# An encoder layer on one core: retention's values for two heads at a time, the heads' projections dealt anew, first loads on another queue, last store in two

## The chip, the cores and the metric

The kernel runs on one core of one Trainium2 chip. A core has a matrix engine (TensorE, PE in the profile; the loads of its stationary operand are shown as PEld), VectorE (DVE), ScalarE (ACT), GpSimd (POOL) and SyncE (SP). SP only issues DMA transfers here; ACT and POOL issue some beside their work. Each engine runs its own list of instructions in order, and semaphores tie the lists together. The metric is the time of one execution on the device in microseconds (us), lower is better, as the median of several runs.

## The reference, cut to what matters

Two request groups of 256 rows and 1024 features go through the same layer with shared weights: a token mixer of two branches (retention with 4 heads, latent attention with 8 heads), then a convolutional gated MLP. All is in float32. Of the mixer's input projection, the parts that the change deals with:

```python
h = _layernorm(x) * (1.0 + sc1) + sh1
proj = h @ w_in
rq, rk, rv, rg, dq, dkv, kr, gA, gB = jnp.split(proj, offs, axis=-1)
rq = _apply_rope(rq.reshape(B, S, RET_HEADS, RET_QK_DIM), cos_r, sin_r)
rk = _apply_rope(rk.reshape(...), cos_r, sin_r) * (RET_QK_DIM ** -0.5)
rv = rv.reshape(B, S, RET_HEADS, RET_V_DIM)          # 4 heads x 256
ro = _bidirectional_retention(rq, rk, rv, ret_decay_fwd, ret_decay_bwd)
ro = _layernorm(ro).reshape(B, S, RET_V_W) * ret_gn_g
y_a = (jax.nn.silu(rg) * ro) @ w_ret_o
merged = jax.nn.sigmoid(gA) * y_a + jax.nn.sigmoid(gB) * y_b
```

The layer ends with `x = _layernorm(ALPHA * x + (1 + g2) * y) * ln2_g + ln2_b`, which is stored. The vectors `sc1`, `sh1`, `g1` and so on are pieces of `silu(c) @ w_ada + b_ada`, where `c` is one row per group.

## The kernel before, in words

Both groups are treated as one matrix of T = 512 rows. The normalized and modulated input `hT` is held transposed: 8 tiles of 128 features x 512 rows (NK = 8). Every float32 operand of a large product is split into a rounded high part and a low rest (`split`, names ending in `_h` and `_l`): ScalarE casts the high part (L151), VectorE subtracts it (L141). A product is then three matmuls (`mm3`, L161 to L163).

Weights are loaded by SP in chunks of 128 x 2048 (1 MB) into two raw buffers (`w_raw`, L192), and split into two high and two low buffers (`w_split`). So a chunk's load waits for the split of the chunk before the last, and its split for TensorE's end with that chunk.

Retention runs in a stage of its own after the attention branch:

- `ret_proj(h)` for a head: a chunk `wqk` gives query and key (2 x 8 x 3 matmuls 512 wide, then `rope` and a split), a chunk `wrv` gives the values, a chunk `wrg` gives the gate (`ps_rg`, then Silu on ScalarE).
- For the values the rows are the stationary operand and the weights stream past: for each of 4 blocks of 128 rows and 8 k, `mm3` into 256 columns of a PSUM tile, one head's width. Two row blocks share a tile `ps_rv` of 512 columns.
- `ret_core(h)` is the head itself: scores (`ps_rs`) times decay gives `sd`, split into `sds`; times values gives `ps_ro`; statistics on VectorE (`lnr_st`), a power on POOL (`lnr_rs`), normalization on ScalarE (`ro`); one head later (for the last head at once) `ret_flip` transposes (`ps_rt`), multiplies with the gate (`rg`, L984) and splits into `roT`.

`interleave(main, filler, ratio)` writes down the steps of a core and, between them, pieces of a filler: the projections of the next head, and for the last head the columns of gate A (`gate_a`, `ps_ga`). Each step yields a cost, and the filler runs until its sum is `ratio` times that of the core. `with_later` also puts in, about every 5 units of cost, a piece of `later`: the adaptive vectors of the second half of the layer, computed on VectorE from loads `araw` (`acc`, L489 and L491) and summed by TensorE (`ps_sum`).

TensorE follows this written order. The order of the other engines, of SP's transfers too, is set by a scheduler from the same program; they then run it in order. PSUM has 8 tiles of 512 columns that all share.

After the last head come the products with `w_ret_o` (`ps_ya`, chunk `wro`); the first two of these take k = 0 to 5 first, and k = 6 and 7, the last head's `roT`, at the end.

At the start SP issues two loads of `c` (`c16`, L173 and L174), the bias rows `b_rows` (L178), then `x` in eight tiles (L223) and `w_ada` in pieces of 256 KB (`wada`, L229). TensorE first runs `ps_warm` matmuls on ones, the transposes `ps_c` of `c16s` and `b_rows`, 16 more `ps_warm`, and then the transposes of `x` (`ps_xt`) between `ps_ada`, products with `wada`. At the end, for each block of 128 rows, VectorE scales (L1383), scales and shifts (L1386) two tiles of 512 columns, and each is stored as it is ready, the first by SP, the second by ACT (L1387).

Of the kernel before, what the change touches and what calls it, by code (L numbers as in the profile page):

```python
# [109 lines left out]
def encoder_kernel(ctx: ExitStack, tc: tile.TileContext, ins, outs):  # L110
# [62 lines left out]
    nc.sync.dma_start(c16[0:8], ins["c_prompt"].rearrange("o (k p) -> (o k) p", p=128))  # L173
    nc.sync.dma_start(c16[8:16], ins["c_sample"].rearrange("o (k p) -> (o k) p", p=128))  # L174
# [3 lines left out]
    nc.sync.dma_start(b_rows, ins["b_ada"].rearrange("o (k p) -> (o k) p", p=128))  # L178
# [342 lines left out]
    with tc.manual_schedule(engines={PE}):  # L521
# [375 lines left out]
        ret = {}  # L897

        def ret_proj(h):
            def pieces(raw):  # L900
# [11 lines left out]
            wv = k_cols(w_in, 0, NK, OFF_RV + h * 256, 256, f"wrv{h}")
            v = []
            for tp in range(2):
                ps = ps512(f"ps_rv{h}_{tp}")
                for i in range(2):
                    t = 2 * tp + i
                    for k in range(NK):
                        mm3(ps[:, i * 256:(i + 1) * 256], cut(hT[k], slice(None), slice(t * 128, t * 128 + 128)),
                            cut(wv, slice(None), k), k == 0, k == NK - 1)  # L920
                v.append(split(ps, f"rv{h}_{tp}"))
                yield 5.2
            wg = k_cols(w_in, 0, NK, OFF_RG + h * 256, 256, f"wrg{h}")
            rg = []
# [12 lines left out]
        def ret_scores(h, g):  # L937
            q, k, _, _, dec = ret[h]
# [37 lines left out]
        def ret_flip(h):  # L976
            for e in range(2):
# [5 lines left out]
                rg = ret[h][3][e]  # L983
# [388 lines left out]
        for t in range(4):  # L1372
# [11 lines left out]
            for cc in range(2):  # L1384
                y = x2[t][cc]
                dve.scalar_tensor_tensor(out=y, in0=y, scalar=rs, in1=ln2b[cc], op0=ALU.mult, op1=ALU.add)  # L1386
                (nc.scalar if cc else nc.sync).dma_start(dst[:, cc * 512:(cc + 1) * 512], y)  # L1387
# [25 lines left out]
```

## Time and profile before

| what | us |
|---|---|
| runs shown | 868.7, 872.14, 1428.62 |
| their median | 872.14 |
| the profiled execution | 868.35 |
| its span in the profile | 866.5 |
| busy: TensorE, VectorE, ScalarE, POOL | 851.8, 612.2, 380.0, 93.3 |

The profile is one execution, recorded by the hardware. A row of a timeline reads: start, length, engine, line of the code, operation, output and inputs, shapes, count, and in brackets the idle time before it with what ended it. Matmuls overlap in the records, since a next one starts before the last has drained; their pace is read from the distance of starts. A row of grouped instructions gives count, total busy time, mean length in ns. In the chain of waits each piece has its start, its length and the engine or transfer that held the end at that moment.

### The profile page before, as it was taken

What the parts mean: (1) busy time and instruction counts of PE and PEld (TensorE: products, weight loads), DVE (VectorE), ACT (ScalarE), POOL (GpSimd) and SP (SyncE); (2) the same over time, 40 slices, a digit from 0 to 9 for tenths busy, and PEclk for the clock granted to TensorE, in tenths of its full rate; (3) what the DMA queues carried; (4) which work ended last, traced back from release to release, by engine and by line L of the source; (5) the groups of instructions that cost most, each with busy time, mean ns of one, the idle gap of its engine ahead of it and who ended that gap; (6) DMA issues with size and microseconds to landing.
All of it is one profiled execution on the core that took longest, in us unless ns stands there. A gap on an engine that the chain in (4) does not pass through costs nothing.

```text
span 866.5 us, 11686 instructions
## 1 busy us (share of the span) xinstructions
PE 851.8 (98%) x4401; PEld 720.8 (83%) x4401; DVE 612.2 (71%) x1051; ACT 380.0 (44%) x647; POOL 93.3 (11%) x141
## 2 busy tenths in 40 slices
PE   8999999999999999999999999999999999999996
PEld 5678888988889898988788899888888888888885
DVE  5465888884677787883986967578657756855666
ACT  3564877551343433453343166434433535443500
POOL 3031012362000000000010210000000000100100
PEclk9999999999999999999999999999999999999998
DMA  9943156799466425354358423245343464655731
GB/s 289 355 153 110 50 153 182 198 294 277 121 168 204 112 98 158 100 185 162 118 187 234 145 82 101 74 146 158 96 147 122 148 181 134 149 167 156 261 112 66
DMA packets 131528, 137.64 MB, mean 159 GB/s; under 512 B 8741, under 2 KB 100227, under 8 KB 131472
## 3 DMA queue, kind: packets, MB, share of 16 engines
q1 hardware_dynamic: 120864, 112.65, 41.5%
q0 software_dynamic: 9888, 23.14, 11.8%
q10 hardware_dynamic: 720, 1.11, 0.3%
q8 instruction: 34, 0.56, 0.3%
q14 instruction: 22, 0.18, 0.1%
HBM read 129.53 MB, written 22.03 MB: 175 GB/s over the span
## 4 chain that ended last, share of the span: by engine, by line
PE 91%; DVE 2%; ACT 2%; DMA 2%; issue 1%; SPq 1%; DVEq 0%; ACTq 0%
PE ps_b L161 5%; PE ps_b L163 5%; PE ps_b L162 5%; PE ps_a L162 5%; PE ps_a L163 5%; PE ps_a L161 5%; PE ps_d L163 4%; PE ps_d L162 4%; PE ps_d L161 4%; PE ps_rv L162 2%; PE ps_rv L163 2%; PE ps_rv L161 2%; PE ps_rqk L161 2%; PE ps_rqk L163 2%; PE ps_rqk L162 2%; PE ps_rg L161 2%
## 5 line engine op out<-in xcount | busy, mean ns | idle before, releaser
L491 DVE SCALAR_TENSOR_TENSOR acc<-araw,csil,acc 128x512 f32<-128x512 f32 x112 | 78.4, 747 | 19.8 <-DMA araw<-in_w_ada_dram 19.8
L161 PE MATMUL ps_b<-h_h,wup_h 128*128 128x512 f32 (+1 forms) x200 | 72.8, 364 | 0.3 <-ACT h2m L401 0.3
L162 PE MATMUL ps_a<-h_l,wup_h 128*128 128x512 f32 (+1 forms) x200 | 72.9, 365 | 0.1
L163 PE MATMUL ps_a<-h_h,wup_l 128*128 128x512 f32 (+1 forms) x200 | 72.8, 364 | 0.0
L161 PE MATMUL ps_a<-h_h,wup_h 128*128 128x512 f32 (+1 forms) x200 | 72.8, 364 | 0.0
L163 PE MATMUL ps_b<-h_h,wup_l 128*128 128x512 f32 (+1 forms) x200 | 72.7, 364 | 0.0
L162 PE MATMUL ps_b<-h_l,wup_h 128*128 128x512 f32 (+1 forms) x200 | 72.7, 364 | 0.0
L141 DVE TENSOR_TENSOR wup_l<-wup_r,wup_h 128x1024 fp32r<-128x1024 f32 (+1 forms) x46 | 52.7, 1173 | 10.2 <-ACT wup_h L151 9.4
L151 ACT CAST wup_h<-wup_r 128x1024 fp32r<-128x1024 f32 (+1 forms) x46 | 44.2, 1014 | 29.8 <-PE ps_b L162 20.2
L144 DVE TENSOR_TENSOR conv<-conv,ps_b 128x512 f32<-128x512 f32 x22 | 15.1, 686 | 40.6 <-PE ps_b L163 37.0
L161 PEld LDWEIGHTS ps_b<-h_h,wup_h 128*128 128x128 f32 x200 | 37.7, 189 | 6.4 <-ACT h2m L401 0.5
L162 PEld LDWEIGHTS ps_a<-h_l,wup_h 128*128 128x128 f32 x200 | 37.7, 189 | 6.2 <-DVE h_l L141 0.3
L163 PEld LDWEIGHTS ps_a<-h_h,wup_l 128*128 128x128 f32 x200 | 37.7, 189 | 6.2 <-DVE wup_l L141 0.3
L162 PEld LDWEIGHTS ps_b<-h_l,wup_h 128*128 128x128 f32 x200 | 37.7, 189 | 6.0
L163 PEld LDWEIGHTS ps_b<-h_h,wup_l 128*128 128x128 f32 x200 | 37.7, 189 | 5.9
L161 PEld LDWEIGHTS ps_a<-h_h,wup_h 128*128 128x128 f32 x200 | 37.7, 189 | 5.9
L162 PE MATMUL ps_rv<-wrv_l,h_h 128*128 128x256 f32 x128 | 36.2, 283 | 0.0
L163 PE MATMUL ps_rv<-wrv_h,h_l 128*128 128x256 f32 x128 | 36.2, 283 | 0.0
L161 PE MATMUL ps_rv<-wrv_h,h_h 128*128 128x256 f32 x128 | 36.2, 283 | 0.0
L1194 ACT ACTIVATE conv<-ps_a,vecs 128x512 f32<-128x512 f32 x22 | 17.1, 779 | 41.8 <-PE ps_a L163 41.8
L1196 DVE SCALAR_TENSOR_TENSOR conv<-ps_a,vecs,conv 128x510 f32<-128x510 f32 x22 | 16.4, 746 | 23.8 <-ACT conv L1194 23.8
L1200 ACT ACTIVATE conv<-conv 128x512 f32<-128x512 f32 x22 | 13.9, 631 | 40.7 <-DVE conv L1198 40.7
(383 smaller groups left out, 2480.6 us busy)
## 6 DMA issues: line engine op xcount, KB each, us to landing
wup_r<-in_w_up_dram SPq DMA_DIRECT2D x44, 512.0 KB, 5.3
araw<-in_w_ada_dram SPq DMA_DIRECT2D x64, 256.0 KB, 5.9
wsum<-in_w_down_dram POOLq DMA_DIRECT2D x42, 256.0 KB, 7.6
wada<-in_w_ada_dram SPq DMA_DIRECT2D x32, 256.0 KB, 6.3
w_r<-wsum SPq DMA_DIRECT2D x28, 256.0 KB, 3.7
wga_r<-in_w_in_dram SPq DMA_DIRECT2D x4, 1024.0 KB, 5.4
wmo_r<-in_w_mla_o_dram SPq DMA_DIRECT2D x4, 1024.0 KB, 5.2
wqk_r<-in_w_in_dram SPq DMA_DIRECT2D x8, 512.0 KB, 5.4
```

Of the source, the lines that this page charges most:

```text
L141: return (eng or dve).tensor_tensor(out=out, in0=a, in1=b, op=ALU.subtract)
L144: (eng or dve).tensor_tensor(out=out, in0=a, in1=b, op=ALU.mult)
L151: last_split.append(act.copy(hi, src).ins)
L161: pe.matmul(out, l[0], r[0], start=start, stop=False, skip_group_check=skip)
L162: pe.matmul(out, l[0], r[1], start=False, stop=False, skip_group_check=skip)
L163: pe.matmul(out, l[1], r[0], start=False, stop=stop, skip_group_check=skip)
L491: dve.scalar_tensor_tensor(out=acc[g], in0=raw, scalar=s, in1=acc[g], op0=ALU.mult, op1=ALU.add)
L1194: act.activation(a, pa, AF.Identity, scale=convw[:, 1, f:f + 1], bias=convb[:, f:f + 1])
L1196: dve.scalar_tensor_tensor(out=av_[:, :, 1:256], in0=pv[:, :, 0:255], scalar=convw[:, 0, f:f + 1], in1=av_[:, :, 1:256], op0=ALU.mult, op1 ...
L1200: act.activation(a, a, AF.Gelu)
```

## The change

- The values are computed for two heads in one go: `ret_value(h)` for h = 0 and 2 loads two chunks of 4 k x 512 columns (`wrv0_0`, `wrv0_4`), keeps four PSUM tiles open, one for each block of rows, and streams 512 columns, two heads' width, in each matmul. A tile of 128 rows x 512 is split, and each head later takes its 256 columns of it (`value_r`).
- `ret_proj` keeps query and key only; the gate is `ret_gate(h)`.
- What runs beside which head is dealt by a table `beside`. Before, head h had the whole projection of head h + 1, and the last head gate A's columns. Now the first core has query and key of head 1 and the gates of heads 1 and 2, the second query and key of head 2 and the values of heads 2 and 3, the third query, key and gate of head 3 and a chunk of gate A, the last two chunks of gate A. The ratios are 6.0, 6.0, 6.0 and 4.6 instead of 6.0 three times and 7.0.
- The two loads of `c` and that of `b_rows` are issued by ACT instead of SP.
- For the last block of rows the second 512 columns are finished and stored in two halves, the first stored by ACT, the second by SP.

```diff
-FILL_MLA, FILL_RET = 0.46, 7.0
+FILL_MLA, FILL_RET = 0.46, (6.0, 6.0, 6.0, 4.6)
...
-    nc.sync.dma_start(c16[0:8], ins["c_prompt"].rearrange("o (k p) -> (o k) p", p=128))
+    nc.scalar.dma_start(c16[0:8], ins["c_prompt"].rearrange("o (k p) -> (o k) p", p=128))
...
-            wv = k_cols(w_in, 0, NK, OFF_RV + h * 256, 256, f"wrv{h}")
-            v = []
-            for tp in range(2):
-                ps = ps512(f"ps_rv{h}_{tp}")
-                for i in range(2):
-                    t = 2 * tp + i
-                    for k in range(NK):
-                        mm3(ps[:, i * 256:(i + 1) * 256], cut(hT[k], slice(None), slice(t * 128, t * 128 + 128)),
-                            cut(wv, slice(None), k), k == 0, k == NK - 1)
-                v.append(split(ps, f"rv{h}_{tp}"))
-                yield 5.2
+            ret[h] = qk[0], qk[1], decay_tile(h)
+
+        def ret_value(h):
+
+            pss = [ps512(f"ps_rv{h}_{t}") for t in range(4)]
+            for k0 in (0, 4):
+                wv = k_cols(w_in, k0, 4, OFF_RV + h * 256, 512, f"wrv{h}_{k0}")
+                for t in range(4):
+                    for k in range(4):
+                        mm3(pss[t], cut(hT[k0 + k], slice(None), slice(t * 128, t * 128 + 128)),
+                            cut(wv, slice(None), k), k0 + k == 0, k0 + k == NK - 1)
+                    if k0:
+                        values[h, t] = split(pss[t], f"rv{h}_{t}")
+                    yield 2.7
+            for i in range(2):
+                value_r[h + i] = [cut(values[h, t], slice(None), slice(i * 256, i * 256 + 256)) for t in range(4)]
...
-        drain(with_later(ret_proj(0)))
+        drain(with_later(chain(ret_proj(0), ret_value(0), ret_gate(0))))
+        beside = [(ret_proj(1), ret_gate(1), ret_gate(2)), (ret_proj(2), ret_value(2)),
+                  (ret_proj(3), ret_gate(3), gate_a(range(EARLY_GA, 2))), (gate_a(range(2, 4)),)]
         for h in range(HR):
-            nxt = ret_proj(h + 1) if h + 1 < HR else gate_a(range(EARLY_GA, 4))
-            interleave(ret_core(h), with_later(nxt), 6.0 if h + 1 < HR else FILL_RET)
+            interleave(ret_core(h), with_later(chain(*beside[h])), FILL_RET[h])
...
-            for cc in range(2):
-                y = x2[t][cc]
-                dve.scalar_tensor_tensor(out=y, in0=y, scalar=rs, in1=ln2b[cc], op0=ALU.mult, op1=ALU.add)
-                (nc.scalar if cc else nc.sync).dma_start(dst[:, cc * 512:(cc + 1) * 512], y)
+            for cc, a, b in ((0, 0, 512), (1, 0, 512)) if t < 3 else ((0, 0, 512), (1, 0, 256), (1, 256, 512)):
+                y = x2[t][cc][:, a:b]
+                dve.scalar_tensor_tensor(out=y, in0=y, scalar=rs, in1=ln2b[cc][:, a:b], op0=ALU.mult, op1=ALU.add)
+                (nc.scalar if cc and not a else nc.sync).dma_start(dst[:, cc * 512 + a:cc * 512 + b], y)
```

How the order of instructions moves, at three places. The first is the head of the DMA lists. SP before (`x0_0` is the first tile of `x`):

```order
L173 DMA c16_77<-in_c_prompt_dram 8x128
L174 DMA c16_77<-in_c_sample_dram 8x128
L178 DMA b_rows_81<-in_b_ada_dram 48x128
L223 DMA x0_0_83<-in_x_prompt_dram 128x512
L223 DMA x0_1_85<-in_x_prompt_dram 128x512
```

ScalarE now, ahead of its first computation (the Silu of `c16`):

```order
L173 DMA c16_77<-in_c_prompt_dram 8x128
L174 DMA c16_77<-in_c_sample_dram 8x128
L176 DMA cst_72<-in_cst_dram 128x128
L178 DMA b_rows_81<-in_b_ada_dram 48x128
L280 ACT_TABLE_LOAD
L280 ACTIVATE c16s_192<-c16_77 16x128
```

The three small loads left SP's list, which now begins with `x0_0`, and stand around the load of `cst` in ScalarE's.

The second place is TensorE's first values, behind the key projection of head 0 (`h0` and `h1` are k = 0 and 1 of `hT`). Before:

```order
L163 MATMUL ps_rqk0_1_2559<-h7_h_657,wqk0_l_2510 128x512
L161 MATMUL ps_rv0_0_2611<-wrv0_h_2605,h0_h_363 128x256
L162 MATMUL ps_rv0_0_2611<-wrv0_l_2606,h0_h_363 128x256
L163 MATMUL ps_rv0_0_2611<-wrv0_h_2605,h0_l_364 128x256
L161 MATMUL ps_rv0_0_2611<-wrv0_h_2605,h1_h_377 128x256
```

and now:

```order
L163 MATMUL ps_rqk0_1_2559<-h7_h_657,wqk0_l_2510 128x512
L161 MATMUL ps_rv0_0_2606<-wrv0_0_h_2612,h0_h_363 128x512
L162 MATMUL ps_rv0_0_2606<-wrv0_0_l_2613,h0_h_363 128x512
L163 MATMUL ps_rv0_0_2606<-wrv0_0_h_2612,h0_l_364 128x512
L161 MATMUL ps_rv0_0_2606<-wrv0_0_h_2612,h1_h_377 128x512
```

Each value matmul streams 512 columns instead of 256; TensorE's list has 192 matmuls fewer in all.

The third place is VectorE at the last head, from the accumulation over `araw` to the low parts of `roT` that `ps_ya` takes last. Before:

```order
L491 SCALAR_TENSOR_TENSOR acc2_1_0_4267<-araw2_1_1_0_4312,csil_194,acc2_1_0_4267 128x512
L984 SCALAR_TENSOR_TENSOR rg3_0_3980<-ps_rt3_0_4357,vecs_235,rg3_0_3980 128x512
L491 SCALAR_TENSOR_TENSOR acc2_1_1_4268<-araw2_1_1_0_4312,csil_194,acc2_1_1_4268 128x512
L984 SCALAR_TENSOR_TENSOR rg3_1_4015<-ps_rt3_1_4367,vecs_235,rg3_1_4015 128x512
L141 TENSOR_TENSOR wro1_l_4388<-wro1_r_4385,wro1_h_4387 128x1024
L491 SCALAR_TENSOR_TENSOR acc2_1_0_4267<-araw2_1_1_1_4316,csil_194,acc2_1_0_4267 128x512
L141 TENSOR_TENSOR wro1_l_4388<-wro1_r_4385,wro1_h_4387 128x1024
L491 SCALAR_TENSOR_TENSOR acc2_1_1_4268<-araw2_1_1_1_4316,csil_194,acc2_1_1_4268 128x512
L141 TENSOR_TENSOR roT6_l_4364<-rg3_0_3980,roT6_h_4363 128x512
L141 TENSOR_TENSOR roT7_l_4374<-rg3_1_4015,roT7_h_4373 128x512
```

and now:

```order
L491 SCALAR_TENSOR_TENSOR acc2_1_0_4044<-araw2_1_1_0_4120,csil_194,acc2_1_0_4044 128x512
L491 SCALAR_TENSOR_TENSOR acc2_1_1_4045<-araw2_1_1_0_4120,csil_194,acc2_1_1_4045 128x512
L491 SCALAR_TENSOR_TENSOR acc2_1_0_4044<-araw2_1_1_1_4124,csil_194,acc2_1_0_4044 128x512
L491 SCALAR_TENSOR_TENSOR acc2_1_1_4045<-araw2_1_1_1_4124,csil_194,acc2_1_1_4045 128x512
L992 SCALAR_TENSOR_TENSOR rg3_0_3740<-ps_rt3_0_4155,vecs_235,rg3_0_3740 128x512
L992 SCALAR_TENSOR_TENSOR rg3_1_3795<-ps_rt3_1_4165,vecs_235,rg3_1_3795 128x512
L141 TENSOR_TENSOR wro1_l_4196<-wro1_r_4193,wro1_h_4195 128x1024 x2
L141 TENSOR_TENSOR roT6_l_4162<-rg3_0_3740,roT6_h_4161 128x512
L141 TENSOR_TENSOR roT7_l_4172<-rg3_1_3795,roT7_h_4171 128x512
```

The accumulations that stood between the products with the gate and the low parts now stand ahead of both, among them those on the second `araw` of this pair. In TensorE's list, 36 gate matmuls stand between the last `ps_ro` and the transposes `ps_rt3` instead of 48. In SP's list the `wo` load stands between the first and the second pair of `araw` of that piece, where it stood ahead of both.

More of the change, by code (lines that the diff above doesn't have):

```diff
@@ L172, in encoder_kernel @@
     c16 = cpool.tile([16, 128], F32, name="c16")
-    nc.sync.dma_start(c16[0:8], ins["c_prompt"].rearrange("o (k p) -> (o k) p", p=128))
-    nc.sync.dma_start(c16[8:16], ins["c_sample"].rearrange("o (k p) -> (o k) p", p=128))
+    nc.scalar.dma_start(c16[0:8], ins["c_prompt"].rearrange("o (k p) -> (o k) p", p=128))
+    nc.scalar.dma_start(c16[8:16], ins["c_sample"].rearrange("o (k p) -> (o k) p", p=128))
     first = _CWHERE["ident"][1]
@@ L177, in encoder_kernel @@
     b_rows = cpool.tile([6 * NK, 128], F32, name="b_rows")
-    nc.sync.dma_start(b_rows, ins["b_ada"].rearrange("o (k p) -> (o k) p", p=128))
+    nc.scalar.dma_start(b_rows, ins["b_ada"].rearrange("o (k p) -> (o k) p", p=128))
     ident = C["ident"]
@@ L894, in out_b @@
                     yield 5.2
-        ret = {}
+        ret, values = {}, {}
         def ret_proj(h):
@@ L911, in ret_proj, with ret_gate @@
                 yield 5.2
[L912 to L922 removed]
+            ret[h] = qk[0], qk[1], decay_tile(h)
[12 more added lines that the diff above has]
+                value_r[h + i] = [cut(values[h, t], slice(None), slice(i * 256, i * 256 + 256)) for t in range(4)]
+        gate_r, value_r = {}, {}
+        def ret_gate(h):
             wg = k_cols(w_in, 0, NK, OFF_RG + h * 256, 256, f"wrg{h}")
[L924 removed]
+            gate_r[h] = []
             for i in range(2):
@@ L929, in ret_proj @@
                 act.activation(s, ps, AF.Silu)
-                rg.append(s)
+                gate_r[h].append(s)
                 yield 5.2
-            ret[h] = (qk[0], qk[1], v, rg, decay_tile(h))
         roT = [None] * NK
@@ L937, in ret_scores @@
         def ret_scores(h, g):
-            q, k, _, _, dec = ret[h]
+            q, k, dec = ret[h]
             ps = ps512(f"ps_rs{h}_{g}")
@@ L948, in ret_out @@
         def ret_out(h, g):
-            s, v = sd.pop((h, g)), ret[h][2]
+            s, v = sd.pop((h, g)), value_r[h]
             ps = ps512(f"ps_ro{h}_{g}")
@@ L954, in ret_out @@
                     mm3(o, cut(s, slice(None), slice(kt * 256 + qt * 128, kt * 256 + qt * 128 + 128)),
-                        cut(v[g], slice(None), slice(kt * 256, kt * 256 + 256)), kt == 0, kt == 1)
+                        v[2 * g + kt], kt == 0, kt == 1)
             if g == 0:
@@ L982, in ret_flip @@
                                      ron[h, g][:, qt * 256 + e * 128:qt * 256 + e * 128 + 128], ident)
-                rg = ret[h][3][e]
+                rg = gate_r[h][e]
                 dve.scalar_tensor_tensor(out=rg, in0=ps, scalar=gret[:, 2 * h + e:2 * h + e + 1], in1=rg,
```

## The prediction

> **What bounds the kernel now.** I read the page first (engine shares, and the slices with the granted clock), then TensorE's waits, TensorE's busy time by stage, and the timelines of the three places that the change touches.
>
> ```profile
> PE 851.8 (98%) x4401; PEld 720.8 (83%) x4401; DVE 612.2 (71%) x1051; ACT 380.0 (44%) x647; POOL 93.3 (11%) x141
> DMA  9943156799466425354358423245343464655731
> ```
>
> TensorE is busy for 98% of the span; the second row, the DMA engines' busy share in 40 slices, is full in the first two slices and again in the ninth and tenth. TensorE's waits by releaser after the start (us in total, times, longest), and its busy time by stage (columns: stretch, length, busy time of PE, PEld, DVE, ACT, POOL, clock, DMA share, GB/s):
>
> ```profile
> PE ps_ya L162 <- DVE roT_l L141: 0.3, 1, 0.3
> ```
>
> ```profile
> 231.00:300.00 69.00, 69.00 (x423) 62.11 (x422) 54.30 (x86) 30.14 (x43) 3.83 (x6) 1.00 0.55 156
> 300.00:371.00 71.00, 71.00 (x438) 64.00 (x437) 54.75 (x98) 28.52 (x45) 3.07 (x3) 1.00 0.40 124
> 371.00:410.00 39.00, 39.00 (x196) 33.06 (x195) 25.32 (x42) 15.85 (x25) 1.63 (x2) 1.00 0.46 150
> ```
>
> From 231 to 410 us, which is all of retention after the first query and key projection, TensorE has no idle time at all, and the granted clock is 1.00. So a matmul that costs less there shortens the kernel by what it saves, as long as nothing that TensorE waits for comes later. VectorE (54 of 69 us) and the weights' loads are covered there, but VectorE's cover is not large. What is left outside TensorE's stream is the start, the end, and one stall of `ps_ya`.
>
> **Values, two heads at a time.** A busy time of a matmul overlaps the next, so I price by the distance of starts. TensorE's timeline, the 256-wide value matmuls (83 rows, the first and the last), and 512-wide ones of two other places (25 rows of `ps_ga`, 20 of `ps_f`):
>
> ```profile
> 230.84 0.28 PE L161 MATMUL ps_rv<-wrv_h,h_h 128*128 128x256 f32 x1
> ...
> 240.67 0.28 PE L162 MATMUL ps_rv<-wrv_l,h_h 128*128 128x256 f32 x1
> ```
>
> ```profile
> 383.81 0.39 PE L163 MATMUL ps_ga<-h_h,wga_l 128*128 128x512 f32 x1
> ...
> 389.25 0.39 PE L163 MATMUL ps_ga<-h_h,wga_l 128*128 128x512 f32 x1
> ```
>
> ```profile
> 459.69 0.39 PE L161 MATMUL ps_f<-wo_h,mg_h 128*128 128x512 f32 x1
> ...
> 464.00 0.39 PE L162 MATMUL ps_f<-wo_l,mg_h 128*128 128x512 f32 x1
> ```
>
> A 256-wide one takes (240.67-230.84)/82 = 0.1199 us, a 512-wide one (389.25-383.81)/24 = 0.2267, and in `ps_f`, where weights stream past stored activations as they do for the values, (464.00-459.69)/19 = 0.2268. Before there are 3 x 128 = 384 value matmuls (x128 on each of three lines); after, two pairs of heads x 4 row blocks x 8 k x 3 = 192. Saved: 384 x 0.1199 - 192 x 0.2267 = 46.04 - 43.53 = **2.5 us**, bounds 2.4 and 2.6 by the rounding of the rows. The Trainium skill ("TensorE: Matmul & The Clock Gate", section "Wait — 56ns, not 53.3ns?") gives a warm matmul N / 2.4 GHz plus about 2.5 ns; by it two 256-wide ones cost only 2.5 ns more than one 512-wide, and 192 x 2.5 ns = 0.5 us would be the estimate of the saving. The rows show 2 x 119.9 - 226.7 = 13 ns, so I stay with 2.5 us.
>
> Splits stay as many (four 2048-column chunks, eight 512-column value tiles), and the loads of `wrv` stay four of 1 MB; how long these took to land here:
>
> ```profile
> DMA to landing us min/median/max: 5.4/6.0/14.4
> ```
>
> Each chunk has the 48 matmuls of the chunk before it, 10.9 us, as cover for its load and its casts; if that cover went, `wrv0_4` would be late first. Cost: nothing. Four PSUM banks of values instead of one or two at a time: TensorE's rows show no wait for a bank now; beside the four, two `ps_ro` and one `ps_rqk` are held at once, seven of eight, so nothing; upper bound 0.7 us, one more VectorE operation of 512 columns, if a bank is freed late.
>
> **The order dealt anew.** Where the profile shows the one stall of this stage, at the first product with `roT_l`, the rows of TensorE, VectorE and the DMA queue are:
>
> ```profile
> 397.28 0.28 PE L161 MATMUL ps_ro<-rv_h,sds_h 128*128 128x256 f32 x1
> ...
> 409.62 1.03 PE L981 MATMUL ps_rt<-cst,ro 128*128 128x128 f32 x8
> ...
> 418.67 0.39 PE L161 MATMUL ps_ya<-roT_h,wro_h 128*128 128x512 f32 x1
> 419.36 0.50 PE L162 MATMUL ps_ya<-roT_l,wro_h 128*128 128x512 f32 x1 [0.30 <-DVE roT_l L141]
> ```
>
> ```profile
> 399.52 0.76 DVE L960 BATCH_NORM_STATS2 lnr_st<-ps_ro 128x6 f32<-128x256 f32 x2
> ...
> 408.60 0.88 DVE L489 TENSOR_SCALAR acc<-araw,csil 128x512 f32<-128x512 f32 x2 [5.45 <-DMA araw<-in_w_ada_dram]
> 411.05 2.08 DVE L491 SCALAR_TENSOR_TENSOR acc<-araw,csil,acc 128x512 f32<-128x512 f32 x3 [1.57 <-DMA araw<-in_w_ada_dram]
> 413.05 0.74 DVE L984 SCALAR_TENSOR_TENSOR rg<-ps_rt,vecs,rg 128x512 f32<-128x512 f32 x1
> ...
> 416.82 1.22 DVE L141 TENSOR_TENSOR wro_l<-wro_r,wro_h 128x1024 fp32r<-128x1024 f32 x1
> ...
> 418.62 1.29 DVE L141 TENSOR_TENSOR roT_l<-rg,roT_h 128x512 fp32r<-128x512 f32 x2
> ```
>
> ```profile
> 401.43 0.37 SPq L192 DMA_DIRECT2D wo_r<-in_w_out_dram  x1
> ```
>
> The starts lie 0.69 apart where 0.23 is due: a stall of 0.46 us. Its cause is VectorE's order: `acc` waits for `araw` in front of `rg`, and two `acc` and two `wro_l` stand between `rg` and `roT_l`. In the order of the changed kernel all the `acc` in between stand ahead of `rg`, the last of them on the pair of `araw` just behind the `wo` load. I put the place on the clock of this profile with the last `ps_ro` held at 397.28 (estimates, from rows). TensorE has 36 gate matmuls behind it instead of 48, so the transposes end 2.7 us earlier and `roT_l` is wanted at 416.1 for the one tile and 416.8 for the other. The `wo` load waits for the second half of `wro_l`: the buffer of `wro0` is free at the end of `ps_ga5`, now 4.2 us ahead of that `ps_ro`, and a cast (1.0), `wro_l` (1.2), two `acc` (1.4), two statistics (0.7) and `wro_l` (1.2) follow, so the load moves from 401.4 to 398.6. Two `araw` landed 7.2 and 9.6 us after it here (408.60 and 411.05), so 405.8 and 408.2; two `acc` to 409.6, two `rg` to 411.0, two `wro_l` to 413.4, two `roT_l` at 414.0 and 414.7. That is 2 us in time, so the 0.46 goes: **0.5 us** gained, with 0 as the other bound. What is late next there is the same `araw`, if it comes over 2 us later than this.
>
> Added waits. The casts of ScalarE on which two of them rest, from rows of other places (two casts of 1024 columns, two of 512, four `ro`):
>
> ```profile
> 384.06 2.01 ACT L151 CAST wga_h<-wga_r 128x1024 fp32r<-128x1024 f32 x2 [0.79 <-PE ps_ga L162]
> ...
> 387.00 1.14 ACT L151 CAST accp_h<-acc 128x512 fp32r<-128x512 f32 x2
> ```
>
> ```profile
> 403.18 1.93 ACT L973 ACTIVATE ro<-ps_ro,lnr_nb,lnr_rs 128x256 f32<-128x256 f32 x4 [3.88 <-DVE lnr_nb L968]
> ```
>
> The casts of `wrg2` now stand ahead of the cast of `sds0_1` and wait for the end of the key projection `ps_rqk1_1`; `ps_ro0_1` waits for `sds0_1`. Two casts (2.0), one of 512 (0.6) and at most two VectorE operations as long as `wro_l` (2.4) are 5.0 us, against the 12 short and 24 long matmuls ahead of `ps_ro0_1`, 1.4 + 5.4 = 6.9 us. Nothing. Tightest is `ps_sum3_0`, which TensorE now meets right behind `ps_rg2_0`. From the end of `ps_rg1_1` on ScalarE does two casts, four `ro` and two `accp_h`, 5.1 us, and VectorE the last `accp_l`, 0.6 (half the `roT_l` row): 5.7, against 24 + 3 matmuls, 6.1 us. 0.4 us of room: cost nothing, upper bound 1.5 us if `araw`, which `accp` needs, lands late.
>
> **The small first loads.** The DMA queue of SyncE and the chain of waits at the start:
>
> ```profile
> 0.74 0.40 SPq L173 DMA_DIRECT2D c<-in_c_prompt_dram  x1
> 1.19 0.28 SPq L174 DMA_DIRECT2D c<-in_c_sample_dram  x1
> ...
> 1.88 1.84 SPq L223 DMA_DIRECT2D x<-in_x_prompt_dram  x4
> ```
>
> ```profile
> 5.79 6.66 DMA wada<-in_w_ada_dram
> ...
> 12.81 3.00 PE ps_ada L371 x8
> ...
> 17.95 1.12 PE ps_ada L371 x8
> ```
>
> Without the three, the `x` loads start at 0.74 instead of 1.88: 1.14 us earlier. The chain runs through loads that come back to back (8 `ps_ada` take 3.00 us at 12.81 and 1.12 at 17.95, so the first wait for them), and they move with the first. What moves to ScalarE's queue must not be late in its place:
>
> ```profile
> 5.34 0.23 PE L296 MATMUL ps_c<-cst,c16s 16*128 16x16 f32 x1
> ...
> 5.69 3.95 PE L291 MATMUL ps_warm<-ones 128*128 128x512 f32 x16
> 10.79 0.33 PE L420 MATMUL ps_xt<-cst,x 128*128 128x128 f32 x1 [1.14 <-ACT x L336]
> ```
>
> Sixteen warming matmuls follow `ps_c` up to 9.64, and `ps_xt` waits 1.14 us behind them for `x`; with `x` 1.14 us earlier that idle time is just used up. VectorE's copies of `ps_c` now stand behind the second pair of `x` statistics, some 0.3 us in the way of the first normalization, which the later wait for `wada` covers. `cst` and `b_rows` are issued behind two more on ScalarE's queue, some 0.8 us behind `c` (0.40 and 0.28 and the gaps) and, with the 1.9 us that `cst` takes to land (its row stands below), still ahead of `ps_c` at 5.34. I take **1.0 us**, nearer to 1.14 than to 0, since the wait that ends last is that for the loads; bounds 0.3 and 1.14.
>
> **The last store in two.**
>
> ```profile
> 861.11 1.41 DVE L1386 SCALAR_TENSOR_TENSOR x<-x,ln_rs,ln2b 128x512 f32<-128x512 f32 x2
> ```
>
> ```profile
> out_dram<-x ACTq DMA_DIRECT2D x4, 256.0 KB, 2.1
> ...
> cst<-in_cst_dram ACTq DMA_DIRECT2D x1, 64.0 KB, 1.9
> ```
>
> The last 512 columns become two operations, 0.05 to 0.1 us longer together (a 512-wide starts 0.66 behind the last, a half I put at 0.36 and 0.42). The last store is half as large: between 1.9 (64 KB) and 2.1 us (256 KB) to land, 2.0. Gain **0.1 us**, bounds -0.1 and 0.2.
>
> **The sum.** 2.5 + 0.5 + 1.0 + 0.1 = 4.1 us from the profiled execution's 868.35 (span 866.5 and 1.85 around it): 864.3. The shown runs are 868.7, 872.14 and 1428.62; the profiled one lies 0.35 below the lowest and 3.8 below the median, so a median of new runs may sit anywhere up to 3.8 above the sum; with the two that agree I add half of 0.35: **864.5 us**.
>
> **Rivals.**
> - A, 0.17: the start gives nothing, since `x`'s loads only queue behind the same bytes or `c16` lands late (for: the DMA engines are full in the first two slices; against: the bytes are the same and begin earlier). 864.5 + 1.0 = 865.5.
> - B, 0.15: a new wait of TensorE, at `ps_sum3_0` or at a value bank, of 0.7 to 1.5 us (for: 0.4 us of room; against: the other places worked out above have 1.9 us and more). About 865.6.
> - C, 0.03, on the other side: VectorE stands at the `araw` ahead of `rg`, and every us beyond 2 is TensorE's at `ps_ya`. Slower than before from 2 + 4.1 = 6.1 us late on. For: a load of `wrv_r` took 14.4 us once against a median of 6.0; so late, it would be 8.4 - 2 = 6.4 us, 870.9. Against: the 64 loads of `araw` landed within 8.3 us.
>
> ```profile
> DMA to landing us min/median/max: 4.8/5.9/8.3
> ```
>
> - D, 0.03: the wide value matmul gives next to nothing: it takes twice 0.1199 in this role, and the 2.5 us stay. 864.5 + 2.5 = 867.0. Against: `ps_f` has the role and takes 0.2268. The formula of the Trainium skill ("TensorE: Matmul & The Clock Gate") that is told above would come out near it, at 866.5 by its estimate; the trace disagrees, by 10 ns a pair.
>
> The forecast itself has 0.62. The range 862.5 to 869.0 takes in A and B, the bounds of the terms (4.4 us at most, 863.9), D, and a run as high above its kin as 872.14 is (864.3 + 3.8 = 868.1); C and a still higher run stay outside. A measurement of this kernel can tell about 2%, 17 us, from no change, and no case reaches that: 0.96 within, 0.02 on either side for what I have not seen.
>
> **What would show it.** Values: 192 rows of 512 columns at 0.227 us. Start: `x` issued near 0.75, `ps_ada` over near 14.7 instead of 15.8. `ps_ya`: no wait for `roT_l`. `ps_sum3_0`: no wait. End: the last landing about 2.0 us after its issue. Wrong would be: any TensorE wait between 220 and 410 us, or `ps_ada` not a us earlier.

## The result, and the profile after

Eight runs of the changed kernel have a median of 865.25 us, eight runs of the kernel before beside them one of 871.19. One of these eight took 1428.62 us; without it the ratio of changed to before is 0.9946, 95% interval 0.9928 to 0.9964. A second set of runs gave 865.68 against 868.25, ratio 0.9957 (0.9941 to 0.9973). So the change saves about 4 us, half a per cent: less than the 2% from which a difference counts here, but not nothing. The forecast was 864.5.

The profiled execution of the changed kernel took 865.91 (span 864.1), 2.4 us less than that of before. Its page, engine shares and the DMA engines' busy share in 40 slices:

```profile
PE 849.4 (98%) x4209; PEld 710.7 (82%) x4209; DVE 612.1 (71%) x1052; ACT 379.1 (44%) x647; POOL 95.0 (11%) x141
...
DMA  9943156799465533553358323255343564655731
```

192 matmuls fewer, TensorE busy for 2.4 us less, the other engines as before. TensorE's timeline of the values and what follows:

```profile
230.51 0.39 PE L161 MATMUL ps_rv<-wrv_h,h_h 128*128 128x512 f32 x1
...
252.04 0.39 PE L163 MATMUL ps_rv<-wrv_h,h_l 128*128 128x512 f32 x1
252.41 0.50 PE L502 MATMUL ps_sum<-accp_h,ones 128*128 128x512 f32 x1
253.13 0.50 PE L503 MATMUL ps_sum<-accp_l,ones 128*128 128x512 f32 x1 [0.23 <-DVE accp_l L141]
253.47 0.40 PE L502 MATMUL ps_sum<-accp_h,ones 128*128 128x512 f32 x1
253.86 0.50 PE L503 MATMUL ps_sum<-accp_l,ones 128*128 128x512 f32 x1
254.19 0.39 PE L161 MATMUL ps_rg<-h_h,wrg_h 128*128 128x512 f32 x1
```

The 96 value matmuls of a pair of heads stand (252.04 - 230.51) / 95 = 0.2266 us apart, as forecast. But behind them there is a wait that the forecast did not have: from 252.04 to 254.19 are five distances, 1.13 us at the usual pace, and 2.15 passed. TensorE lost 1.0 us at `ps_sum4_1`, of which the brackets show only 0.23; distances of starts show it all. VectorE's and the DMA queue's rows in front of it:

```profile
244.70 2.08 DVE L491 SCALAR_TENSOR_TENSOR acc<-araw,csil,acc 128x512 f32<-128x512 f32 x3 [2.79 <-DMA araw<-in_w_ada_dram]
...
252.39 1.41 DVE L141 TENSOR_TENSOR accp_l<-acc,accp_h 128x512 fp32r<-128x512 f32 x2
```

```profile
237.96 1.01 SPq L192 DMA_DIRECT2D wqk_r<-in_w_in_dram  x2
239.01 1.91 SPq L485 DMA_DIRECT2D araw<-in_w_ada_dram  x2
```

VectorE is idle for 2.79 us until `araw` lands and has work without a gap from then until `accp_l` is done at 253.8; TensorE wanted the first `accp_l` at 252.5. That `araw` was issued only at 239.01, behind a weight load that had waited for its raw buffer.

The start, TensorE and the DMA issues (KB each, median us from issue to landing):

```profile
1.48 4.21 PE L291 MATMUL ps_warm<-ones 128*128 128x512 f32 x9 [1.48 <-DVE ones L276]
6.98 0.20 PE L296 MATMUL ps_c<-cst,c16s 16*128 16x16 f32 x1 [1.29 <-DMA cst<-in_cst_dram]
7.33 0.26 PE L297 MATMUL ps_c<-cst,b_rows 48*128 48x48 f32 x1 [0.16 <-DMA b_rows<-in_b_ada_dram]
7.52 3.92 PE L291 MATMUL ps_warm<-ones 128*128 128x512 f32 x16
...
12.74 2.68 PE L371 MATMUL ps_ada<-wada,c 128*32 128x512 f32 x8
15.35 0.33 PE L420 MATMUL ps_xt<-cst,x 128*128 128x128 f32 x1
```

```profile
cst<-in_cst_dram ACTq DMA_DIRECT2D x1, 64.0 KB, 5.2
...
b_rows<-in_b_ada_dram ACTq DMA_DIRECT2D x1, 24.0 KB, 5.2
```

The small loads go out by 2.5 us, but beside the eight loads of `x` they take 5.2 us to land, where `cst` took 1.9 before. So `ps_c` starts at 6.98 and 7.33 instead of 5.34 and 5.50, TensorE idles 1.5 us in the middle of its warming, and `ps_ada` is over at 15.35 instead of 15.74: 0.4 us gained, not 1.0. `c16` is late as well: ScalarE waits for it until 5.01 (2.84 before) and has `c16s` at 6.61, so `ps_c` would not have met 5.34 with an early `cst` either. That the traffic of `x` does this, and not the place in ScalarE's queue, is borne out by a load that did not move. The first one on GpSimd's queue goes out at 1.26 before and at 1.27 now; before (first row) and now (second):

```profile
vec_rows<-in_q_norm_g_dram POOLq DMA_DIRECT2D x1, 1.0 KB, 2.1
```

```profile
vec_rows<-in_q_norm_g_dram POOLq DMA_DIRECT2D x1, 1.0 KB, 4.5
```

The Trainium skill ("DMA: Bandwidth & Descriptors", section "Queues, rings and completion order") says that the queues of SyncE and ScalarE are rings on the same 16 DMA engines, which take turns between them packet by packet. The longer landing agrees with that; the turns themselves no run here shows.

At `ps_ya`, VectorE, and TensorE at the first products with the last head's `roT`:

```profile
405.28 2.74 DVE L491 SCALAR_TENSOR_TENSOR acc<-araw,csil,acc 128x512 f32<-128x512 f32 x4 [2.85 <-DMA araw<-in_w_ada_dram]
408.49 1.41 DVE L992 SCALAR_TENSOR_TENSOR rg<-ps_rt,vecs,rg 128x512 f32<-128x512 f32 x2 [0.47 <-PE ps_rt L989]
...
412.08 1.29 DVE L141 TENSOR_TENSOR roT_l<-rg,roT_h 128x512 fp32r<-128x512 f32 x2
```

```profile
416.90 0.39 PE L161 MATMUL ps_ya<-roT_h,wro_h 128*128 128x512 f32 x1
417.13 0.39 PE L162 MATMUL ps_ya<-roT_l,wro_h 128*128 128x512 f32 x1
```

All the `acc` in between stand ahead of `rg` now, and both `roT_l` are there at 413.4. TensorE's first product with one of them starts at 417.13, 0.23 behind the matmul ahead of it: no stall, and some 4 us of room.

At the end, VectorE's last row, the two tiles in three operations:

```profile
858.70 1.53 DVE L1395 SCALAR_TENSOR_TENSOR x<-x,ln_rs,ln2b 128x512 f32<-128x512 f32 x3
```

It takes 0.12 us more than the 1.41 of the kernel before. The span does not end with the store, though. GpSimd and SyncE at the program's last line (duration min/median/max in ns, first and last start in us):

```profile
L1418 POOLq DRAIN  x3: 46/97/5849, 857.5 to 863.9; - x3
...
L1418 SPq DRAIN  x3: 7/7/47, 862.9 to 863.6; - x3
```

GpSimd's first `DRAIN`, 5.85 us from 857.5, is over at 863.35; SyncE's first one, which comes behind the last landing (862.3), begins at 862.9. Before, GpSimd's ended at 865.75 and SyncE's first began at 865.0. What this makes of the term for the store is said at the run with one store.

### The profile page after: what moved, and what is told of

It is laid out like the page before. It is cut to its first block, busy times and chain, and to the rows that moved or that the text cites. A ratio compares the mean times of both kernels' runs of the same rounds, so it can differ in the third digit from the quotient of the medians.

```text
span 864.1 us, 11309 instructions
## 1 busy us (share of the span) xinstructions
PE 849.4 (98%) x4209; PEld 710.7 (82%) x4209; DVE 612.1 (71%) x1052; ACT 379.1 (44%) x647; POOL 95.0 (11%) x141
## 4 chain that ended last, share of the span: by engine, by line
PE 91%; DVE 3%; DMA 2%; ACT 2%; issue 1%; SPq 0%; ACTq 0%; DVEq 0%
PE ps_b L161 5%; PE ps_b L163 5%; PE ps_b L162 5%; PE ps_a L162 5%; PE ps_a L163 5%; PE ps_a L161 5%; PE ps_d L163 4%; PE ps_d L162 4%; PE ps_d L161 4%; PE ps_ga L161 2%; PE ps_ga L162 2%; PE ps_ga L163 2%; PE ps_rg L162 2%; PE ps_rg L163 2%; PE ps_ya L163 2%; PE ps_rg L161 2%
## 5 line engine op out<-in xcount | busy, mean ns | idle before, releaser
L1274 POOL DMA_DIRECT2D x1d<-ux x12 | 10.7, 929 | 175.9 <-DVE ux L144 111.4
L848 POOL DMA_DIRECT2D wsum<-in_w_down_dram x42 | 28.1, 1171 | 7.3 <-DMA wsum<-in_w_down_dram 7.1
L151 ACT CAST w_h<-w_r 128x1024 fp32r<-128x1024 f32 (+1 forms) x20 | 17.9, 944 | 19.2 <-PE ps_d L163 10.2
```

The source lines that it names most:

```text
L151: last_split.append(act.copy(hi, src).ins)
L848: tc.keep_in_program_order(nc.gpsimd.dma_start(dst, src, **kw))
L1274: nc.gpsimd.dma_start(x1_rows(t, c), u, accum_op=ALU.add)
```

## The experiments

Three places of the program are compared across all kernels below, by TensorE's starts: the first `ps_rqk` (all that is ahead of retention; the first 220 us differ from kernel to kernel only at the start), the distance from there to the first `ps_ya` (retention), and from there to the last `ps_d`. "16 warming" is the length of the warming row behind `ps_c`, "ada over" the start of the `ps_xt` behind the first eight `ps_ada`, and "idle at ps_sum" what the starts around `ps_sum` lie apart beyond their pace. All worked out from TensorE's timelines, in us:

| kernel | 16 warming | ada over | first ps_rqk | to first ps_ya | idle at ps_sum | to last ps_d |
|---|---|---|---|---|---|---|
| before | 3.95 | 15.74 | 219.96 | 190.45 | 0 | 447.33 |
| before, again | 4.64 | 15.34 | 219.55 | 192.00 | 1.5 | 447.09 |
| changed | 3.92 | 15.35 | 219.63 | 189.01 | 1.0 | 446.69 |
| changed, again | 5.52 | 15.22 | 219.40 | 188.01 | 0 | 446.65 |
| values narrow | 3.91 | 14.97 | 219.17 | 190.42 | 0 | 446.59 |
| one sum later | 6.47 | 16.56 | 220.70 | 189.94 | 1.9 | 446.58 |
| small loads back | 4.17 | 15.63 | 219.83 | 188.46 | 0.4 | 446.61 |
| ps_c behind | - | 14.53 | 218.70 | 188.37 | 0.3 | 446.58 |
| ps_c behind, araw early | - | 14.83 | 219.04 | 188.95 | 0.9 | 446.65 |
| ps_c behind, two sums later | - | 14.34 | 218.62 | 187.99 | 0 | 446.68 |
| the same, one store | - | 15.04 | 219.30 | 187.99 | 0 | 446.84 |
| warming 5 + 20 | 7.49 (20) | 17.35 | 221.52 | 188.12 | 0.1 | 446.58 |

**The width of the values.** One edit, the loop of the three products:

```diff
-mm3(pss[t], cut(hT[k0 + k], ...), cut(wv, slice(None), k), k0 + k == 0, k0 + k == NK - 1)
+l, r = cut(hT[k0 + k], ...), cut(wv, slice(None), k)
+for n, (x, y) in enumerate(((l[0], r[0]), (l[0], r[1]), (l[1], r[0]))):
+    one = k0 + k == n == 0
+    for c in (slice(0, 512),) if one else (slice(0, 256), slice(256, 512)):
+        pe.matmul(pss[t][:, c], x, y[:, c], start=one, stop=k0 + k == NK - 1 and n == 2, ...)
```

> The changed kernel with its value matmuls cut back to 256 columns in the same place and order (8 stay wide, those that open a PSUM bank; 184 become 368). My theory, that a 256-wide one costs 0.1199 us and a 512-wide one 0.2267: 368 x 0.1199 - 184 x 0.2267 = 44.1 - 41.7 = 2.4 us longer, all of it between the first ps_rqk and the first ps_ya; spacing of 0.120 in the rows, 865.2 + 2.4 = 867.6 as a median. Rival (a matmul costs its columns and next to nothing else): under 0.6 us longer, 865.8, spacing near 0.114.

TensorE's timeline at both ends of the first pair's values:

```profile
230.05 0.39 PE L925 MATMUL ps_rv<-wrv_h,h_h 128*128 128x512 f32 x1
230.28 0.40 PE L925 MATMUL ps_rv<-wrv_l,h_h 128*128 128x256 f32 x2
...
253.05 0.39 PE L502 MATMUL ps_sum<-accp_h,ones 128*128 128x512 f32 x1
```

23.00 us for 4 wide and 184 narrow ones: (23.00 - 4 x 0.2267) / 184 = 0.1201 each. Retention takes 190.42 without any idle time at `ps_sum`, against 187.99 to 188.01 in the three profiles with wide values and no idle time there: 2.4 us, as expected of the theory, and not the 0.6 of the rival. The median is 867.17, 1.7 above the 865.47 of the kernel with the small loads back, which ran beside it. That is less than 2.4. Part of the reason may be that the wide values bring TensorE to `ps_sum4_1` 1.2 us sooner, where it can wait (0.4 us in that kernel's profile), and the narrow ones do not; the two kernels' starts differ as well. No run here parts the two.

**One sum later.** The sums of `ps_sum4_1` one step on, behind `ps_rg0_0`:

```diff
         yield 0.0
         yield 0.0
+        if (which, cc) == (4, 1):
+            yield 0.0
         for g in range(2):
...
-        yield 0.86
+        if (which, cc) != (4, 1):
+            yield 0.86
```

> The changed kernel with the four ps_sum4_1 matmuls one step later on TensorE, behind ps_rg0_0 instead of in front of it (their four loads of araw stay where they are). My theory, that the 1.0 us of idle time at 252 to 254 us is a wait for accp_l, which VectorE finishes 1.2 us too late: the first ps_rqk to the first ps_ya becomes 188.2 - 1.0 = 187.2 us, no wait at ps_sum, 864.2 as a median. Rival (ps_rg0_0 takes over the wait, since wrg_l of the same VectorE queue is late as well): ps_rg waits as long as ps_sum did, and the stage stays 188.2.

Neither held in the profile. The wait at `ps_sum4_1` is gone and `ps_rg` does not wait, but 1.9 us turned up at `ps_sum3_0`. The median is 865.44 (864.51 to 867.83) where 864.2 was expected. The profiled execution, 867.83, is the slowest of the eleven, so its 1.9 us, and its late start, are not what this kernel usually loses. TensorE's waits:

```profile
PE ps_sum L505 <- DVE accp_l L141: 1.2, 1, 1.2
```

VectorE and the DMA queue, ahead of it:

```profile
282.67 1.22 DVE L141 TENSOR_TENSOR wrg_l<-wrg_r,wrg_h 128x1024 fp32r<-128x1024 f32 x1 [0.26 <-ACT wrg_h L151]
...
285.80 1.22 DVE L141 TENSOR_TENSOR wrg_l<-wrg_r,wrg_h 128x1024 fp32r<-128x1024 f32 x1
...
292.93 1.42 DVE L491 SCALAR_TENSOR_TENSOR acc<-araw,csil,acc 128x512 f32<-128x512 f32 x2 [1.12 <-DMA araw<-in_w_ada_dram]
```

```profile
287.04 0.38 SPq L192 DMA_DIRECT2D wrv_r<-in_w_in_dram  x1
287.47 0.98 SPq L485 DMA_DIRECT2D araw<-in_w_ada_dram  x2
```

The edit moves four matmuls, but the scheduler laid out VectorE anew behind them: both halves of `wrg2_l` stand behind `sds0_1_l` now, the second behind two `acc` as well. That half frees the raw buffer for the load of `wrv2_0` (issued 0.02 us after it ends, at 287.04), and the `araw` behind that load on SyncE's queue goes out at 287.47, against 282.14 in the changed kernel (4.3 us later, counted from the first `ps_rqk`). VectorE then waits for it (1.12 us), and `accp_l` is late for TensorE.

**The small loads back.** `nc.scalar.dma_start` to `nc.sync.dma_start` for `c16` (two) and `b_rows`, all else as changed.

> The changed kernel with c and b_rows back on SyncE's queue ahead of x, as before the change. The trace of the changed kernel says the move was worth 0.33 to 0.39 us: first ps_rqk at 219.96 again instead of 219.63, the first eight ps_ada over at 15.7 instead of 15.35, 865.6 as a median. By the prediction's term (1.0) it would be 220.6 and 866.2; if the move was worth nothing, 219.63 stays.

First `ps_rqk` at 219.83, `ps_ada` over at 15.63, median 865.47 (865.02 to 865.59): nothing lost against the 865.25 and 865.68 of the changed kernel. The expectation rested on one profile of each kernel, and its 0.4 us are no more than executions of one start differ by (219.17 to 220.70 in the four with the changed start).

**`ps_c` behind the warming.**

```diff
-keep_warm(WARM_FIRST)
+keep_warm(WARM_FIRST + WARM_THEN)
 pe.transpose(ps[:, :16], c16s, ident[:16, :16])
 pe.transpose(ps[:, 16:16 + 6 * NK], b_rows, ident[:6 * NK, :6 * NK])
-keep_warm(WARM_THEN)
```

> The changed kernel with the two ps_c transposes behind all 25 warming matmuls, so that c16s and b_rows, which now land late, can hold up none of these. Theory 1 (the start ends when the fourth wada load lands, and TensorE's late warming only fills its wait for that): ps_c no longer waits, the idle time in ps_ada grows by as much, ps_ada is over at 15.35 and the first ps_rqk starts at 219.63 as now. Theory 2 (the late small loads hold TensorE's chain and eat the rest of the predicted 1.0): TensorE is 1.2 us earlier through the warming, ps_ada is over 0.4 to 0.7 us earlier, the first ps_rqk at about 219.1.

```profile
1.47 7.30 PE L291 MATMUL ps_warm<-ones 128*128 128x512 f32 x25 [1.47 <-DVE ones L276]
8.71 0.23 PE L296 MATMUL ps_c<-cst,c16s 16*128 16x16 f32 x1
...
11.77 2.83 PE L370 MATMUL ps_ada<-wada,c 128*32 128x512 f32 x8 [0.29 <-DVE c L300]
14.53 0.33 PE L419 MATMUL ps_xt<-cst,x 128*128 128x128 f32 x1
```

Theory 2, and by more than it had (0.4 to 0.7): `ps_ada` over 0.8 us earlier than in the changed kernel, the first `ps_rqk` at 218.70, median 864.48, 1.0 below the kernel with the small loads back. In the four kernels with this start the first `ps_rqk` is at 218.62 to 219.30, on average 218.92. With the start of before it is at 219.78 (three profiles), with the changed start at 219.73 (four). So the early `x` and the later `ps_c` together are worth 0.9 us; the later `ps_c` alone, with the small loads back on SyncE's queue, was not run. With `ps_c` where it was, the early `x` is worth nothing on average. That average hangs on the one execution at 220.70, which lost time in its warming (last section); the other three are at 219.40, 0.4 us ahead of the start of before. Part of theory 1 stays true: the eight `ps_ada` still take 2.83 us here, so they wait for `wada`.

**The changed kernel again.** No edit.

> The changed kernel once more, unedited, beside the next three on one chip, to see how much its start and its wait at ps_sum4_1 differ from one execution to the next. My theory (both hang on when loads land): the first ps_rqk between 219.1 and 220.8, idle time around ps_sum4_1 between 0.2 and 1.1 us, every spacing of the value matmuls the same; 865.3 as a median. Rival (the differences between the runs so far came from their edits): 219.63 and 1.0 us again, within 0.1.

No idle time at all at `ps_sum4_1`, retention 188.01, first `ps_rqk` 219.40: the wait is one of some executions, as the theory had it (0 is a little outside its bound of 0.2). The `araw` whose issue stood at 239.01 goes out 0.9 us earlier here, counted from the first `ps_rqk`, and lands 0.4 us faster. At the start the sixteen warming matmuls took 5.52 us instead of 3.92. Busy time by stretch (length, PE busy, granted clock, DMA share, GB/s):

```profile
5.50:9.00 3.50, 2.05 (x9) 0.96 1.06 339
9.00:13.00 4.00, 4.00 (x13) 0.61 1.09 345
```

The granted clock fell to 0.61 behind the idle time at `ps_c`.

**`araw` early**, on top of `ps_c` behind:

```diff
+ahead = {1: (1, 2), 2: (3,), 3: ()} if (which, cc) == (4, 1) else {}
+raws = {}
 for kq in range(4):
+    for at in ahead.get(kq, (kq,)):
+        for k in range(2):
+            raws[at, k] = t512(F32, f"araw{which}_{cc}_{at}_{k}")
+            nc.sync.dma_start(raws[at, k], w_ada[:, at * 2 + k, col:col + 512])
     for k in range(2):
-        raw = t512(F32, f"araw{which}_{cc}_{kq}_{k}")
-        nc.sync.dma_start(raw, w_ada[:, kq * 2 + k, col:col + 512])
+        raw = raws[kq, k]
...
```

> The kernel with ps_c behind the warming, and the last two pairs of araw of ps_sum4_1 issued one step earlier, ahead of the wqk load on SyncE's queue. My theory (accp_l of ps_sum4_1 is late because that araw is issued behind a weight load that waits for its buffer): no idle time at ps_sum4_1. But the planner lays VectorE out anew behind it as in the run with the later sums, wrg2_l again behind two acc, so the load of wrv2_0 and the araw behind it go out late and TensorE waits 1 to 2 us at ps_sum3_0 instead: first ps_rqk to first ps_ya 189.2 to 190.2 us, about 866 as a median. Rival (the wait at ps_sum3_0 in that run came from one late load, not from the order): neither place waits, the stage is 188.0 to 188.2, 864.2.

The places are those of the theory, the size is not: nothing at `ps_sum4_1`, 0.9 us at `ps_sum3_0` (1 to 2 were expected), retention 188.95, median 864.79. TensorE's waits:

```profile
PE ps_sum L507 <- DVE accp_l L141: 0.5, 1, 0.5
```

The wait at `ps_sum3_0` has now come with the changed order in two kernels. That the early `araw` is what took away the one at `ps_sum4_1` isn't shown, since the unedited kernel had an execution without it too.

**Two sums later**, on top of `ps_c` behind: the edit of "one sum later" with `(which, cc) in ((4, 1), (3, 0))` in both conditions.

> The kernel with ps_c behind the warming, and the sums of ps_sum4_1 and of ps_sum3_0 both one step later on TensorE, behind the next 24 matmuls, with all loads in their places. My theory (both waits are accp_l coming 0.3 to 2 us after TensorE, and the 5.4 us of a step cover that): no idle time from the first ps_rqk to the first ps_ya, that stage 188.1 us, 864.1 as a median, the fastest of these kernels. Rival (the wait moves on to the next that VectorE feeds, ps_rg or ps_rv): the stage stays 188.4 or more.

Retention in TensorE's busy time by stage (columns as in the prediction):

```profile
218.60:406.60 188.00, 188.00 (x913) 158.71 (x912) 145.88 (x244) 78.04 (x116) 9.45 (x11) 1.00 0.49 153
```

188.00 of 188.00 us busy, as the theory had it. Median 864.36 (863.88 to 864.71), against 865.68 (864.24 to 866.59) for the changed kernel on the same chip; ratio to before 0.9942 (0.9928 to 0.9956). Its median is the lowest of all kernels here, though only 0.1 below the next two with `ps_c` behind (864.46 and 864.48), which is no difference. Its runs scatter over 0.8 us instead of 2.4.

**Warming 5 + 20.** `WARM_FIRST, WARM_THEN` from 9, 16 to 5, 20 in the changed kernel: the wait at `ps_c` made longer.

> The changed kernel with 5 warming matmuls ahead of the two ps_c and 20 behind them instead of 9 and 16, so that TensorE idles about 3 us, not 1.3, for cst and b_rows. My theory (the wait for the late small loads can cost the granted clock: in one execution the 16 warming matmuls behind it took 6.5 us instead of 3.9): the 20 behind take about 0.4 us each, 8 us, ps_ada begins near 17.3 and the first ps_rqk at 221.5 to 222.5, median 867 to 868. Rival (that execution was disturbed otherwise, the idle time costs no clock): the 20 take 4.7 us, ps_ada begins near 13.6 and the first ps_rqk is at 219.5 to 220.5.

```profile
6.93 0.25 PE L296 MATMUL ps_c<-cst,c16s 16*128 16x16 f32 x1 [2.96 <-DMA cst<-in_cst_dram]
...
7.55 7.49 PE L291 MATMUL ps_warm<-ones 128*128 128x512 f32 x20
...
16.35 1.06 PE L371 MATMUL ps_ada<-wada,c 128*32 128x512 f32 x8
```

The theory's case, a little less of it: the 20 take 7.49 us where full pace gives 4.7, `ps_ada` starts at 16.35 and no longer waits for loads (1.06 us), the first `ps_rqk` is at 221.52, the median 866.82, 1.1 above the changed kernel on the same chip.

**One store**, on top of the two sums later: the last 512 columns in one operation and one store again.

> The kernel with ps_c behind the warming and both sums a step later, with the last 512 columns of the output as one VectorE operation and one store again. My theory (the split costs VectorE 0.12 us and wins about as much in the landing): from the start of the last ps_d to the end of the span 8.76 to 8.86 us, as in the kernels with the split (8.77 to 8.86 in nine profiles); 864.4 as a median, no difference from the run with the split. By the prediction's term: 0.1 us longer, 8.87 to 8.96.

From the start of the last `ps_d` to the end of the span: 8.77 here and 8.76 in both profiles of the kernel before, against 8.77 to 8.86, on average 8.81, in the nine with the split. The median is 864.46 against 864.36. Those spans are rounded to 0.1 us; by the traces' own times the distance is 8.80 or 8.81 in all twelve profiles, so the split gives nothing at all. GpSimd's `DRAIN` can account for that: in all twelve it begins 2.16 to 2.17 us behind the start of the last `ps_d` and lasts 5.84 to 5.86, and the span ends 0.78 to 0.79 behind it, while SyncE's last `DRAIN` ahead of that end is over 0.3 to 0.7 us sooner. So the end of GpSimd came last and not the store, with or without the split. No run moved GpSimd's end, so what a shorter store would be worth then stays open.

**The kernel before again.** No edit.

> The kernel before, unedited, profiled a second time. My theory (its start hangs on loads that nothing of TensorE delays, and its stall at ps_ya on VectorE's order): no wait at ps_c, the 16 warming matmuls in about 3.95 us, the first ps_rqk between 219.6 and 220.1, 0.4 to 0.7 us of idle time around ps_ya with roT_l, 190.4 us from the first ps_rqk to the first ps_ya. Rival (the start of this kernel is as unsteady as that of the changed one, and its stall at ps_ya came from one late load): the first ps_rqk away from 219.96 by 0.5 or more, no stall at ps_ya.

TensorE's waits:

```profile
PE ps_sum L502 <- ACT accp_h L151: 0.6, 1, 0.6
...
PE ps_sum L503 <- DVE accp_l L141: 0.2, 1, 0.2
PE ps_ya L162 <- DVE roT_l L141: 0.2, 1, 0.2
```

The first `ps_rqk` is 0.05 us outside the expected bounds, nothing waits at `ps_c` (the warming took 4.64, longer than expected), and the stall at `ps_ya` is there again: 0.35 us (starts 0.58 apart where 0.23 is due) where the first profile had 0.46, a little under the expected 0.4 to 0.7. Not expected was the rest: this execution waits 1.5 us at `ps_sum4_1`, and its retention takes 192.00 us instead of 190.45. The wait that looked new in the changed kernel is in the kernel before as well, and the one profile that the forecast was made from happened to be without it.

## Why the prediction was right, and where it was not

- **Values, 2.5 us: right.** 2.4 by undoing the width alone, and 190.45 - 188.00 = 2.45 between the profiles of both kernels that have no idle time at `ps_sum`. The pace of each width, read from rows of other places, was that of the value rows. The rule of the Trainium skill ("TensorE: Matmul & The Clock Gate", section "Wait — 56ns, not 53.3ns?"), by which the estimate of the saving was 0.5 us, does not hold for these rows. Rival D (nothing saved) falls by the same rows.
- **The stall at `ps_ya`, 0.5 us: right.** It is in both profiles of before and in none with the change; from `ps_ya` to the last `ps_d` the two kernels' profiles differ by 447.33 - 446.69 = 0.64 and 447.09 - 446.65 = 0.44 us. No run undoes VectorE's order alone; that it is the cause rests on the rows. There are some 4 us of room instead of the forecast 2, so rival C, whose place this is, had no opening.
- **The start, 1.0 us: wrong.** On average nothing was gained (219.73 against 219.78). The step that failed is the sentence that `cst` and `b_rows`, issued some 0.8 us behind `c`, land "still ahead of `ps_c` at 5.34". It took the 1.9 us that `cst` needed when it went out at 0.73, over a us ahead of the first `x`, and they now travel beside 2 MB of `x`: 5.2 us. The rest of that step was right: `x` was issued at 0.74, and with `ps_c` out of the way the gain is 0.9 us. Rival A named the outcome, and as one of its reasons a late `c16`, which is late too (`c16s` at 6.61 in the first profile).
- **The last store, 0.1 us: not there.** The two halves cost VectorE 0.12 us more than one operation (1.53 instead of 1.41 us for the last tiles), a little above the 0.05 to 0.1 priced; the last landing took the 2.0 us forecast, but begins later, and so comes 0.05 us later behind the last `ps_d` than before (6.93 against 6.87). The step that failed is that the span was taken to end with this store: GpSimd's `DRAIN` ended 0.3 to 0.7 us behind SyncE's in every profile.
- **Added waits, nothing: half right.** `ps_sum3_0` was called the tightest, with 0.4 us of room, and TensorE met it without a wait in all six profiles in which VectorE's order there is that of the changed kernel. In the two that disturb this order and leave the sum in its place it waited 0.9 and 1.9 us just there. But `ps_sum4_1`, 45 us ahead of it, was not worked out at all; the prediction's "other places worked out above" do not hold it. It waited 0 to 1.0 us in the changed kernel, which is rival B's price at a place that B did not name.
- **The sum.** 864.5 stands against 865.25 and 865.68. What is missing is the start and, in some executions, the wait at `ps_sum4_1`: the first profile lost 0.7 us to the one and 1.0 to the other, the second 0.4 and nothing. That the forecast came within 1.2 us also owes something to its base, a profile of before that was faster than most of its runs: from the median shown, 872.14, the same terms give 868.0. The gain over the median of before may be no smaller than forecast because that median also holds waits which this profile did not show; the repeated profile found 1.5 us of them. What the runs of before at 870 us and more contain was not profiled (869.2 was the slowest one seen), so how much of the gain over the median comes from fewer such waits stays open.

## What to carry to other kernels

A load that is moved to an idle queue still shares the DMA engines: take its landing time from a place with the same traffic, not from a place where it was alone, and look at what stands in order behind the first instruction that needs it. Where loads wait for buffers that a second engine frees, and that engine waits in its order for loads of the same queue, lateness goes round: list every point where the bounding engine takes a result of that engine, not only the tightest by estimate, and profile the kernel before twice, since one profile may be one without the wait. An edit that moves four instructions can have a scheduler lay out another engine anew; compare the order before reading a result as that of the edit. Before a last store is made shorter, see which engine's end comes last.

## What the runs showed that was not expected

Some 1.5 us of idle time in the middle of the warming can cost TensorE's clock, in some executions. Behind it the 16 warming matmuls took 3.92, 3.91, 5.52 and 6.47 us in four executions of the same start, and behind 3.0 us of idle time 20 took 7.49. Not all of such a difference is the gap's: without one, the 25 warming matmuls took from 7.30 to 8.85 us in seven executions, as the clock came up sooner or later. With one they took 8.12, 8.13, 9.60 and 10.68, and 9.99 behind the longer gap, so three of five lie above all that have none. One sum later, TensorE:

```profile
7.14 0.26 PE L296 MATMUL ps_c<-cst,c16s 16*128 16x16 f32 x1 [1.47 <-DMA cst<-in_cst_dram]
...
7.78 6.47 PE L291 MATMUL ps_warm<-ones 128*128 128x512 f32 x16
...
15.56 1.06 PE L371 MATMUL ps_ada<-wada,c 128*32 128x512 f32 x8
```

The loads were there long before `ps_ada` began (8 take 1.06 us, none waits), so here the slow warming held the start, by about 1.2 us against the changed kernel's first profile. The Trainium skill ("TensorE: Matmul & The Clock Gate", section "Part 1: The HAM clock gate (the "warmup" mystery)") has the clock rise after a window of some 3.4 us of work, in windows that do not start with the kernel. That the same gap costs nothing in one execution and 2.5 us of warming in another agrees with it; that a gap far shorter than a window is enough is what the rows add. The column with the granted clock shows it in only one of these cases (0.61, above), where the clock had come up and fell again. In this one it had not come up yet, and the column reads 1.00 (columns as above):

```profile
2.00:4.50 2.50, 2.50 (x7) 1.00 0.83 265
9.00:13.00 4.00, 4.00 (x10) 1.00 1.05 328
```

This 1.00 says nothing. The column reads 1.00 in the first stretch too, where nine warming matmuls take 4.21 us, while 16 at the full pace take 3.9. The trace's first record of the clock stands at 13.28 us, just where the pace of the rows doubles, and what lies ahead of the first record is shown as 1.00. In the first microseconds the distance of starts has to be read.
